# Splitting the first load of a row-wise kernel into three: runs of 2, 2 and 60 KiB instead of 2 and 62

## Chip, cores, metric

The kernel runs on one core of one Trainium2 chip. The metric is the device time of one execution in microseconds (us). All times are medians over several runs; profiles are of one execution each.

## What the kernel must compute

```python
# x: float32 [1024, 4096]
mean = np.mean(x, axis=-1, keepdims=True)
return ((x - mean) ** 2).astype(np.float32)
```

16.8 MB are read and 16.8 MB are written. The arithmetic is one sum and one square for each element.

## The kernel before

The 1024 rows are spread over 128 partitions and two tiles. A tile holds four rows on each partition, 64 KiB in one piece of memory. Both tiles have their own buffer, so no load waits for a buffer. All loads are issued first, on SP's queue; the first tile's load is cut in two, a "head" of 512 columns (2 KiB on each partition) and the remainder of 62 KiB.

```python
Q, HEAD = 4, 512                      # rows of a tile on a partition; columns of the head
x_t   = x.rearrange("(p n q) d -> n p (q d)", p=P, q=Q)
out_t = out.rearrange("(p n q) d -> n p (q d)", p=P, q=Q)

tiles = []
for i in range(ntiles):                                   # two tiles
    x_tile = io.tile([P, Q * D], F32)
    cuts = [0, HEAD, Q * D] if i == 0 else [0, Q * D]
    for lo, hi in zip(cuts, cuts[1:]):
        nc.sync.dma_start(out=x_tile[:, lo:hi], in_=x_t[i][:, lo:hi])
    tiles.append(x_tile)

for i in range(ntiles):
    ...   # means and squares in place, shared by ScalarE (ACT) and VectorE (DVE), 17 us a tile
    nc.sync.dma_start(out=out_t[i], in_=tiles[i])
```

## Time and profile before

| | before |
|---|---|
| time, median (first 3 runs) | 83.02 us (83.0 to 83.29) |
| profiled span | 81.4 us |
| DMA bytes, mean rate | 33.55 MB, 412 GB/s |
| DMA queue's share of 16 engines | 95.9% |
| VectorE, ScalarE busy | 41%, 43% |
| first tile landed | 22.51 us |

The prediction below shows the lines. How to read them: the share of the DMA queue is the time its packets took, over the span times 16 DMA engines. A packet here is one run of one partition: 2 KiB, 62 KiB or 64 KiB. In the views cut into 40 slices a packet is counted where it starts. "To landing" is from the start of a DMA's issue to its last semaphore update.

Besides the views I read the trace's packet records: start, duration and size of every packet. They do not name the engine. A packet of 4 bytes is the semaphore write with which an engine ends its part of a transfer, and an engine that goes straight on has its next packet 6 ns after it.

### The profile page before, as it was taken

How to read it: one execution, taken by the hardware profiler on the slowest of the kernel's cores; microseconds unless marked ns; L12 is line 12 of the kernel's file. 1: busy time of each engine (PE TensorE's matmuls, PEld its weight loads, DVE VectorE, ACT ScalarE, POOL GpSimd, SP SyncE). 2: the span in 40 equal slices, each digit the busy share in tenths (PEclk: the TensorE clock that was granted, in tenths of full speed). 3: DMA queues.
4: the chain of work that ended last, by engine and by line, in shares of the span. 5: the costliest groups of instructions: out<-in, count | busy, mean ns of one | idle time of the engine just before them, and what ended most of it. 6: DMA issues, size and time to landing. Idle time of an engine off the chain costs nothing.

```text
span 81.4 us, 83 instructions
## 1 busy us (share of the span) xinstructions
DVE 33.4 (41%) x16; ACT 34.7 (43%) x13; POOL 0.2 (0%) x4
## 2 busy tenths in 40 slices
DVE  0000000000089999999439999999900000000000
ACT  6000000000099999999339999999800000000000
POOL 0000000000000000000000000000000000000000
DMA  1999939999992999993899998399999199999290
GB/s 26 602 499 468 406 156 468 499 499 499 516 451 97 483 516 516 516 483 161 387 516 516 516 483 387 161 516 516 516 516 451 64 516 516 516 516 483 129 419 0
DMA packets 720, 33.55 MB, mean 412 GB/s; under 512 B 80, under 2 KB 80, under 8 KB 208
## 3 DMA queue, kind: packets, MB, share of 16 engines
q1 hardware_dynamic: 720, 33.55, 95.9%
HBM read 16.78 MB, written 16.78 MB: 412 GB/s over the span
## 4 chain that ended last, share of the span: by engine, by line
DMA 49%; DVE 21%; SPq 1%; issue 0%
DMA x_tile<-in_x_dram 49%; DVE neg_sum L67 16%; DVE x_tile L90 2%; DVE x_tile L89 1%; SPq L51 1%; DVE neg_mean L70 1%
## 5 line engine op out<-in xcount | busy, mean ns | idle before, releaser
L67 DVE TENSOR_REDUCE neg_sum<-x_tile 128x1 f32<-128x4096 f32 x6 | 26.5, 4412 | 25.0 <-DMA x_tile<-in_x_dram 25.0
L74 ACT ACTIVATE x_tile<-x_tile,neg_mean 128x4096 f32<-128x4096 f32 (+1 forms) x8 | 26.0, 3324 | 0.1
L59 ACT ACTIVATE copy<-x_tile 128x4096 f32<-128x4096 f32 x2 | 7.2, 3617 | 23.1 <-DMA x_tile<-in_x_dram 23.1
L90 DVE TENSOR_TENSOR x_tile<-x_tile 128x1792 f32<-128x1792 f32 x2 | 4.1, 2026 | 0.1
L89 DVE TENSOR_SCALAR x_tile<-x_tile,neg_mean 128x1792 f32<-128x1792 f32 x2 | 2.3, 1153 | 0.1
L59 ACT ACT_TABLE_LOAD x1 | 1.3, 1283 | 0.7 <-PEq L108 0.7
L70 DVE TENSOR_SCALAR neg_mean<-neg_sum 128x1 f32<-128x1 f32 x6 | 0.9, 154 | 0.2
L59 ACT ACTIVATION_READ_ACCUMULATOR copy<-x_tile 128x1 f32 x2 | 0.4, 186 | 0.0
L108 POOL MEMSET const-bfloat16-1.0<- 128x1 bf16 x1 | 0.1, 102 | 0.0
L108 POOL MEMSET const-uint8-127<- 128x1 uint8 x1 | 0.1, 101 | 0.0
L108 POOL MEMSET const-float32-0.0<- 128x1 f32 x1 | 0.1, 99 | 0.2 <-issue 0.2
L108 POOL MEMSET const-float32-1.0<- 128x1 f32 x1 | 0.1, 98 | 0.0
## 6 DMA issues: line engine op xcount, KB each, us to landing
x_tile<-in_x_dram SPq DMA_DIRECT2D x1, 7936.0 KB, 21.4
x_tile<-in_x_dram SPq DMA_DIRECT2D x1, 256.0 KB, 2.6
out_dram<-x_tile SPq DMA_DIRECT2D x2, 21.7
x_tile<-in_x_dram SPq DMA_DIRECT2D x1, 40.2
```

What stands on the lines that cost most here:

```text
L51: nc.sync.dma_start(out=x_tile[:, lo:hi], in_=x_t[i][:, lo:hi])
L59: nc.scalar.activation(out=copy, in_=row, func=ACT.Identity, scale=-inv_d, accum_out=neg_mean)
L67: inorder(nc.vector.reduce_sum(out=neg_sum, in_=row, axis=mybir.AxisListType.X, negate=True))
L70: inorder(nc.vector.tensor_scalar_mul(out=neg_mean, in0=neg_sum, scalar1=inv_d))
L74: inorder(nc.scalar.activation(out=part, in_=part, func=ACT.Square, bias=neg_mean, scale=1.0))
L89: nc.vector.tensor_scalar_add(out=back, in0=back, scalar1=m2)
L90: nc.vector.tensor_mul(out=back, in0=back, in1=back)
L108: nc = _bacc.Bacc("TRN2", target_bir_lowering=False, num_devices=1)
```

## The change

The intent is a longer run-in of small transfers before the big one. The bytes, the order and all compute stay as they are.

```diff
-        cuts = [0, HEAD, Q * D] if i == 0 else [0, Q * D]
+        cuts = [0, HEAD, 2 * HEAD, Q * D] if i == 0 else [0, Q * D]
```

The first tile has three loads: two heads of 2 KiB and a remainder of 60 KiB on each partition. The remainder is now the third issue on SP.

## The prediction

> **What bounds the kernel now.** I read the page first for busy shares, then the chain of waits, then the waits of SP's queue, and last the DMA view in short windows.
>
> The page, its slices and its DMA part:
>
> ```profile
> DVE 33.4 (41%) x16; ACT 34.7 (43%) x13; POOL 0.2 (0%) x4
> ...
> DVE  0000000000089999999439999999900000000000
> ACT  6000000000099999999339999999800000000000
> ...
> DMA  1999939999992999993899998399999199999290
> ...
> DMA packets 720, 33.55 MB, mean 412 GB/s; under 512 B 80, under 2 KB 80, under 8 KB 208
> ...
> q1 hardware_dynamic: 720, 33.55, 95.9%
> ```
>
> No compute engine is busy half of the span, while the one DMA queue fills 95.9% of the time of 16 DMA engines. 33.55 MB is x read once (16.78 MB) and the output written once. The low digits in the DMA row are an artefact: packets here last more than one slice and are counted where they start.
>
> The chain of waits, which starts from the last instruction (a VectorE one that ends at 58.8 us):
>
> ```profile
> 1.64 40.24 DMA x_tile<-in_x_dram
> 41.88 0.02 issue
> 41.90 4.43 DVE neg_sum L67
> ...
> 56.76 2.02 DVE x_tile L90
> ```
>
> Its chain runs through the second tile's load. It stops at 58.8 us and misses the last store, which the waits of SP's queue show:
>
> ```profile
> SPq L91 <- DVE x_tile L90: 55.0, 2, 36.1
> SPq L122 <- DMA out_dram<-x_tile: 21.2, 2, 19.3
> ```
>
> The program ends by waiting for the second store. The question is whether the DMA engines ever run dry before it. The timeline of SP's queue, with the landing times of the page's DMA issues, answers it:
>
> ```profile
> 0.73 1.33 SPq L51 DMA_DIRECT2D x_tile<-in_x_dram  x3
> 39.56 19.64 SPq L91 DMA_DIRECT2D out_dram<-x_tile  x2
> ...
> x_tile<-in_x_dram SPq DMA_DIRECT2D x1, 7936.0 KB, 21.4
> x_tile<-in_x_dram SPq DMA_DIRECT2D x1, 256.0 KB, 2.6
> out_dram<-x_tile SPq DMA_DIRECT2D x2, 21.7
> x_tile<-in_x_dram SPq DMA_DIRECT2D x1, 40.2
> ```
>
> Store 0 is issued at 39.56 us; the second load lands only at 41.88. Store 1 is issued at 58.85 (39.56 + 19.64, less its own 0.35); store 0 lands at 39.56 + 21.7 = 61.3. Each store is queued over 2 us before the transfer ahead of it has landed. So the four transfers follow each other without a hole, and the end is the first packet's time plus the sum of the packets on the slowest DMA engine. Compute can move by some tenths of a microsecond without moving the end.
>
> The speed inside a transfer comes from the DMA view of 5.1 to 21.4 us, where all packets are 62 KiB runs:
>
> ```profile
> DMA packets 112, 7.11 MB, mean 436 GB/s; under 512 B 0, under 2 KB 0, under 8 KB 0
> ...
> q1 hardware_dynamic: 112, 7.11, 100.6%
> ```
>
> 1.006 x 16.3 us x 16 engines / 112 packets = 2.342 us for 63,488 bytes, 27.1 bytes per ns on an engine, 434 GB/s on 16.
>
> The same view of 2.45 to 2.65 us, inside the first head:
>
> ```profile
> DMA packets 34, 0.07 MB, mean 348 GB/s; under 512 B 0, under 2 KB 0, under 8 KB 34
> ...
> q1 hardware_dynamic: 34, 0.07, 89.2%
> ```
>
> 0.892 x 0.2 us x 16 / 34 = 84 ns for 2,048 bytes, 24.4 bytes per ns. A short run costs a little over 10% more per byte than a long one.
>
> **What the Trainium skill says.** "DMA: Bandwidth & Descriptors", section "Where 436 GB/s comes from", puts the ceiling at 16 x 32 bytes x 850 MHz = 435 GB/s. The 434 GB/s above agrees: the long runs have nothing left to gain. The same page, "Why a DMA increments its semaphore by 16 and not by 1", says a tile of 128 partitions is spread over 16 engines, each with its own semaphore write. The trace agrees: 5 transfers and 80 packets under 512 B, 16 for each. The same page, "Latency and other measured facts", gives about 600 ns to a first byte for this kind of queue; the packet records put the first packet at 1.74 us, 0.63 us after the first issue ended at 1.11 us. "Perfetto Trace Analysis", section "DMA Optimizations", says that splitting DMAs may let work start sooner if the engines are generally idle. They are not idle here.
>
> **The change part by part.**
> 1. One more issue on SP. The three issues of loads stand at 0.73, 1.16 and 1.64 us (the chain of waits and the packet records' issue list agree), about 0.45 us apart. The big remainder of tile 0 is now issued third, at 1.64, not at 1.16. The first issue at 0.73 led to a first packet at 1.74, so 1.01 us; the remainder is ready at about 2.65 us. The second load moves to about 2.11 us, with nothing to do until some 21 us. Cost on the path: zero if the engines still have work at 2.65 us.
> 2. They have. The first head's closing semaphore writes lie at 2.66 to 3.01 us in the packet records. The second head, issued at 1.16 and so ready at about 2.2 us, follows with 8 packets of 84 ns on each engine: 0.67 us, to 3.3 to 3.7 us. The remainder has been waiting for 0.7 us or more by then.
> 3. 2 KiB of each partition move from a long run to a short one. On each engine: 8 x 84 ns = 672 ns for 16,384 bytes, against 16,384 / 27.1 = 604 ns before. That is +68 ns.
> 4. One more semaphore write on each engine, 9 ns in the packet records: +9 ns.
> 5. No compute instruction changes: the order of VectorE and ScalarE is the same. Tile 0 is still waited for as a whole by the first reduction (row 0 reaches past both heads) and by the mean of row 3, so the second head lets nobody start earlier.
>
> Sum on the path: 0.07 + 0.01 = **+0.08 us**, so 83.02 + 0.08 = 83.10 us.
>
> **Rivals.**
> - *A hole after the heads, because three issues come late.* For it: SP needs 0.45 us for each issue, and one head alone moves its steady part in 0.67 us an engine. Against it: step 2. If the remainder came up as late as 4 us there would be a hole of 0.3 to 0.6 us, and 83.4 to 83.7 us.
> - *A better start.* The first head runs at 220 GB/s on average from 1.7 to 2.66 us, and the first long packets average about 2.62 us in the packet records where later ones take 2.34: some 0.28 us is lost on each engine. If a longer run-in of short packets spared the long ones this, the time would be 82.8 to 82.9 us. For it: the existing head suggests that somebody found it worth having. Against it: the short packets already run at a steady 84 ns at the end of the first head, so nothing is left to warm up in the second; I expect the long packets' loss to be only moved later.
> - *Luck of the slowest engine.* The 16 engines end the first tile between 21.50 and 22.19 us and the last store between 79.67 and 80.21 us: the engine that lost most in its first long packet (2.99 us) plausibly stays last to the end. The mean of the last writes is 79.82, so the worst engine is 0.39 us behind. Another start deals this afresh: plus or minus 0.3 us.
> - *A store that misses its place.* Tile 0 landing later moves store 0's issue by as much, but also the second load. The store would be ready about 1.0 us after its issue, 40.6 us, and the first engine finishes the load at 40.84, the slowest at 41.58. The slack of the slowest, which sets the end, is 1 us. A delay of 0.08 on both sides takes nothing from it.
>
> **Range and chances.** The runs before span 83.0 to 83.29, so 0.3 us is noise or dealing of the start. Around 83.10 I take 0.25 below (the better start) and 0.4 above (a small hole, a worse slowest engine): 82.85 to 83.5. Two per cent is 1.66 us; no step above reaches half of it, so within 2% gets 0.98 and each side 0.01.
>
> **What would show it.** In the changed page: 864 packets (720 + 128 + 16), 96 under 512 B, 352 under 8 KB, a queue share still near 96%, a span near 81.5 us. Among the DMA issues: two of 256 KB landing about 2.6 and 2.9 us after issue, and one of 7680 KB about 21 us after its own. VectorE's first reduction starts near 22.7 us against 22.61. Store 0 is issued near 39.65. Steps 1 and 2 are wrong if no packet runs for some tenths of a microsecond between 2.7 and 4 us; step 3 is wrong if the second head's packets do not take about 84 ns; the second rival is right if the first long packets come close to 2.27 us (61,440 / 27.1) and tile 0 lands earlier than 22.5 us. The prediction as a whole fails if a store or the second load starts only after the engines have gone dry.

## The result

The changed kernel took **85.81 us** (85.35 to 85.86, 6 runs), the kernel before 83.16 (83.0 to 83.38, 6 runs). The ratio is 1.0304, 95% interval 1.0274 to 1.0335: slower by 3%. (A ratio here is the mean time of one kernel's runs over that of the other's of the same rounds, so not quite the ratio of the medians.) Executions over 1.5% slower than the fastest of the same kernel are left out of the means.

The changed kernel's page, its engine and DMA part:

```profile
DVE 33.4 (40%) x16; ACT 34.7 (41%) x13; POOL 0.2 (0%) x4
...
DMA packets 864, 33.55 MB, mean 399 GB/s; under 512 B 96, under 2 KB 96, under 8 KB 352
...
q1 hardware_dynamic: 864, 33.55, 94.3%
```

The packet counts are those predicted. Busy times of the engines are unchanged, and so is the work; only the span grew, from 81.4 to 84.0 us.

Its chain of waits, with the part that was shown of before:

```profile
1.64 0.42 SPq L51
2.06 0.04 issue
2.10 42.51 DMA x_tile<-in_x_dram
44.62 0.02 issue
44.64 4.43 DVE neg_sum L67
```

Its timeline of SP's queue, with the DMA issues of its page:

```profile
0.73 1.81 SPq L51 DMA_DIRECT2D x_tile<-in_x_dram  x4
42.35 19.59 SPq L91 DMA_DIRECT2D out_dram<-x_tile  x2
...
x_tile<-in_x_dram SPq DMA_DIRECT2D x1, 7680.0 KB, 23.6
x_tile<-in_x_dram SPq DMA_DIRECT2D x2, 256.0 KB, 2.8
out_dram<-x_tile SPq DMA_DIRECT2D x2, 21.6
x_tile<-in_x_dram SPq DMA_DIRECT2D x1, 42.5
```

Read against the lines of before: the remainder takes 23.6 us to land, where 62 KiB runs took 21.4. It is issued 0.47 us later too, so tile 0 is there at 1.64 + 23.63 = 25.27 us instead of 22.51. The second load lands at 44.62 instead of 41.88 (+2.74), and the last store, by the landing records, at 83.25 instead of 80.56 (+2.69). The stores take what they took. So the whole loss arises before 25 us, in the load of the first tile, and nothing later gives it back.

Now the start in a narrow window. This is the DMA view of the changed kernel from 3.8 to 5.6 us. Its second heads had ended on every engine by 3.745 us (last semaphore write in the packet records):

```profile
DMA  0000000000000090000900000000000990009900
...
DMA packets 7, 0.43 MB, mean 239 GB/s; under 512 B 0, under 2 KB 0, under 8 KB 0
```

Seven packets begin here: 0.43 MB / 7 = 61 KB, so they are long ones. The packet records give their starts as 4.43, 4.69, 5.23, 5.25, 5.28, 5.42 and 5.51 us. These are the first packets of the remainder on 7 of the 16 engines, which had nothing to do for 1.7 us on average: the last writes of their own heads lie at 3.16 to 3.60 us. The other nine went on without a gap at 3.20 to 3.75 us.

The same view of the kernel before, from 3.1 to 5.1 us (its head ends by 3.013 us):

```profile
DMA packets 0, 0.00 MB, mean 0 GB/s; under 512 B 0, under 2 KB 0, under 8 KB 0
```

No packet begins, because all 16 engines are inside the first long packet that they began at 2.67 to 3.02 us, each 5 to 6 ns behind its head.

There is a second symptom. The changed kernel from 5.8 to 9.3 us, when all engines have work:

```profile
DMA packets 19, 1.17 MB, mean 334 GB/s; under 512 B 0, under 2 KB 0, under 8 KB 0
...
q1 hardware_dynamic: 19, 1.17, 100.1%
```

1.001 x 3.5 us x 16 / 19 = 2.95 us for one packet of 60 KiB. Later the same packets take 2.267 us in the packet records. In this stretch the nine early engines are in their second packet, 3.43 us on average. The seven late ones spend 3.15 us on their first.

**The sum for the engine that ends last.** Before, its first long packet began at 2.82 us; after, at 5.51. Of this 2.68 us, 0.68 is the second head (8 x 84 + 9 ns), as predicted; **2.0 us is the hole**, by difference. Its eight long packets took 16.37 + 2.99 = 19.37 us before and 19.44 after: 8 x 0.075 = 0.60 less for the shorter runs, and **0.68 us more because more of them are slow** (1.33 us over the normal in sum, against 0.65). 0.68 - 0.60 + 2.0 + 0.68 = 2.76 us, which is the later landing of tile 0.

### The profile page after: what moved, and what is told of

Read it like the earlier page. It is cut to its first block, busy times and chain, and to the rows that moved or that the text cites. A ratio compares the mean times of both kernels' runs of the same rounds, so it can differ in the third digit from the quotient of the medians.

```text
span 84.0 us, 85 instructions
## 1 busy us (share of the span) xinstructions
DVE 33.4 (40%) x16; ACT 34.7 (41%) x13; POOL 0.2 (0%) x4
## 4 chain that ended last, share of the span: by engine, by line
DMA 51%; DVE 20%; SPq 1%; issue 0%
DMA x_tile<-in_x_dram 51%; DVE neg_sum L67 16%; DVE x_tile L90 2%; SPq L51 1%; DVE x_tile L89 1%; DVE neg_mean L70 1%
## 6 DMA issues: line engine op xcount, KB each, us to landing
x_tile<-in_x_dram SPq DMA_DIRECT2D x1, 7680.0 KB, 23.6
```

## The experiments

Each was run beside the kernel before on the same chip, with three rounds of timing. The diffs show the lines that matter, against the kernel before; those of e8 and e9 are against the changed kernel. A descriptor, in what follows, is the record of one run that a DMA engine is to move. An engine counts as late if its first long packet of the remainder begins after the last semaphore write of the short loads ahead of it. The first data of every run but e15 move at 1.73 to 1.81 us.

| run | remainder issued at, us | short loads end by, us | late engines | median, us | ratio to before (95%) |
|---|---|---|---|---|---|
| kernel before | 1.16 | 3.01 | 0 | 83.16 | |
| changed | 1.64 | 3.75 | 7 | 85.81 | 1.0304 (1.0274, 1.0335) |
| e16: changed again | 1.63 | 4.08 | 6 | 85.41 | 1.0259 (1.0200, 1.0319) |
| e1: one head, 4 KiB | 1.17 | 3.98 | 0 | 83.25 | 0.9996 (0.9914, 1.0077) |
| e2: second head issued third | 1.15 | 3.14 | 0 | 83.26 | 0.9986 (0.9921, 1.0051) |
| e9: second head on ACT's queue | 1.16 | 4.08 | 0 | 83.23 | 0.9984 (0.9918, 1.0049) |
| e11: one head, two runs | 1.21 | 4.18 | 0 | 83.59 | 1.0039 (1.0002, 1.0076) |
| e17: remainder delayed by half | 1.44 | 3.10 | 1 | 83.42 | 1.0055 (1.0015, 1.0096) |
| e14: remainder delayed | 1.70 | 3.09 | 14 | 84.82 | 1.0182 (1.0113, 1.0251) |
| e5: tiny load between | 1.55 | 3.14 | 2 | 85.39 | |
| e13: 2, 4, 58 KiB | 1.64 | 4.94 | 1 | 84.30 | 1.0133 (1.0095, 1.0172) |
| e15: tiny load first (data at 2.10) | 1.53 | 3.44 | 1 | 83.46 | 1.0048 (0.9969, 1.0127) |
| e7: 2, 14, 48 KiB | 1.63 | 7.63 | 0 | 83.06 | 0.9971 (0.9902, 1.0039) |
| e6: 14, 2, 48 KiB | 1.64 | 7.57 | 0 | 83.10 | 0.9971 (0.9891, 1.0050) |
| e8: second tile issued late | 1.63 | 3.76 | 9 | 85.41 | 1.0240 (1.0170, 1.0311) |

The count of late engines is a lower bound, because an engine whose own head ended early can wait before that last write. If each first long packet is paired with a semaphore write 5 to 6 ns before it, those left without a partner are 7 in the changed kernel, 7 in e16, 9 in e8, 15 in e14, 5 in e5, 3 in e15, 2 in e17 and one each in e13 and e2, none in the other rows. The one in e2 waited 0.17 us.

Not in the table, because their loads are not comparable: e0 (no head), e12, the first attempt at e14, and e19 (the three loads in mid-run).

### First call: is it the sizes, the number of loads, or the place of the remainder?

Theory A: the remainder is issued too late. Theory B: two heads fill what an engine's queue holds. Theory C: runs of 60 KiB are slow in themselves. Theory D: four outstanding loads are too many.

**e1_head_4k**

```diff
-        cuts = [0, HEAD, Q * D] if i == 0 else [0, Q * D]
+        cuts = [0, 2 * HEAD, Q * D] if i == 0 else [0, Q * D]
```

> One head of 4 KiB per partition, remainder issued second (60 KiB runs, as in the changed kernel). Theory A (the remainder is issued third, so its descriptors reach some DMA engines late, under load): no hole, 83.1 to 83.3 us. Theory B (the queue of a DMA engine holds few descriptors, and two heads of 8 fill it): no hole either, 8 descriptors ahead, 83.1 to 83.3. Theory C (60 KiB runs or a start of 4 KiB into the row are what runs slowly): 85.5 to 86.

Measured 83.25 us, the same as before. C is out: the remainder has the same 60 KiB runs from the same column, and each of its first packets takes 2.267 us (one 2.278).

**e2_head2_third** (the changed kernel's three loads, in another order)

```diff
+        parts = [(0, HEAD), (2 * HEAD, Q * D), (HEAD, 2 * HEAD)] if i == 0 else [(0, Q * D)]
```

> The changed kernel's three loads of tile 0, with the second head issued third, after the 60 KiB remainder. A and B: the remainder is second again, no hole, 83.1 to 83.4 us. C: 85.5 to 86. Theory D (four loads outstanding instead of three are too many, whatever their order): 85 to 86.

Measured 83.26 us, the same as before. D is out: all the loads of the changed kernel are there, 864 packets too. What helps is that the remainder is second.

**e4_one_dma_two_runs** (the 4 KiB head of e1, its access pattern written as two runs of 2 KiB)

```diff
+            if i == 0 and lo == 0:
+                to = to.rearrange("p (r c) -> p r c", c=HEAD)
+                of = of.rearrange("p (r c) -> p r c", c=HEAD)
```

> One head whose 4 KiB per partition are written as two runs of 2 KiB; if the access pattern is kept, the page shows 256 packets of 2 KiB and the DMA engines have 16 descriptors of data ahead of the remainder, as in the changed kernel, but one issue fewer. A: 83.1 to 83.3 us. B: a hole, 85 to 86 us. If the page shows 128 packets of 4 KiB, the pattern was merged and this run repeats e1.

Measured 83.37 us, but the page has 720 packets: the two adjacent runs were merged, so this repeats e1 and says nothing on B. e11 mends it.

**e5_tiny_between** (the kernel before, with a load of 512 bytes to one partition of a spare tile between head and remainder)

```diff
+            if i == 0 and lo == HEAD:
+                spare = scratch.tile([1, 128], F32)
+                nc.sync.dma_start(out=spare, in_=x[0:1, 0:128])
```

> The kernel before with a load of one partition and 512 bytes (one DMA engine, into a spare tile) issued between the head and the remainder: the remainder is issued third, at about 1.6 us, but 15 of 16 engines have only the first head's 8 descriptors ahead of it. A: late descriptors, some engines start the remainder past 4 us, 84.5 to 86 us. B: 83.1 to 83.4 us. D: 85 to 86 us.

Measured 85.53, 85.3, 83.62 and 85.47 us. The three higher runs lie over 1.5% above the fourth, so there is no ratio. The trace is of a high run (85.53); it has late engines, but there is no trace of the run at 83.62. Its DMA view from 3.2 to 4.5 us, after the last head ended at 3.14:

```profile
DMA packets 2, 0.13 MB, mean 98 GB/s; under 512 B 0, under 2 KB 0, under 8 KB 0
```

Two engines begin the remainder late, at 3.67 and 4.16 us. They are not the engine that had the extra transfer: in the packet records the 512-byte packet begins at 2.901, its semaphore write at 2.925 and a long packet at 2.931 us, without a gap. So one more transfer in an engine's own queue did not make that engine late, which speaks against B. What all engines share is a remainder issued at 1.55 us.

### Second call: how much must stand ahead of a remainder that is issued third?

**e6_long_short_rest**

```diff
+        cuts = [0, 7 * HEAD, 8 * HEAD, Q * D] if i == 0 else [0, Q * D]
```

> Three loads of tile 0 with runs of 14, 2 and 48 KiB. The remainder is issued third at 1.64 us, as in the changed kernel, but the first load keeps the engines busy to about 6 us. Theory B2 (a DMA engine's queue is supplied with two transfers at a time; the third is supplied only when the first is finished on it, and that takes 1 to 2 us): the 0.7 us of the second load do not hide it, so some engines idle about 1 us after it, near 6.5 to 8 us, and the time is 84.3 to 86 us. Theory A2 (the supply of the third transfer starts at its issue and is slow only beside the start of the others, done by 5.5 us): no hole, 83.1 to 83.4 us.

Measured 83.10 us, the same as before. The remainder's packets begin at 7.23 to 7.57 us, each right behind its engine's second load. B2 is out: here too the remainder is third and the load ahead of it is 2 KiB.

**e7_short_long_rest**

```diff
+        cuts = [0, HEAD, 8 * HEAD, Q * D] if i == 0 else [0, Q * D]
```

> Runs of 2, 14 and 48 KiB. The remainder is third, but the second load lasts some 4 us from 2.8 us on, longer than the late supply of the changed kernel (5.5 us at the latest). B2 and A2 both: no hole, 83.1 to 83.4 us. A theory that three loads of one tile, or four outstanding loads, cost 2.5 us in themselves: 85 to 86 us.

Measured 83.06 us, the same as before. Three loads of a tile cost nothing in themselves.

**e8_tile1_late** (the changed kernel, the second tile's load held back by a GpSimd fill of its buffer)

```diff
+        if i == 1:
+            nc.gpsimd.memset(x_tile[:, 0:2 * D], 0.0)
```

> The changed kernel, with the second tile's load issued only after a GpSimd fill of half of its tile (some us, to be landed long before 20 us). Theory F (the second tile's load, issued 0.45 us after the remainder, is what holds the remainder's supply back or slows its first packets): no hole and no slow packets, 83.1 to 83.4 us. B2 and A2: nothing changes, 85.3 to 86 us.

Measured 85.41 us. The second tile was issued at 7.68 us, and nine engines were late all the same, one of them by 0.07 us only (at 3.83 us). The DMA view of this run, 3.9 to 5.6 us, shows the other eight:

```profile
DMA  0000000000000000000009999990009000000000
...
DMA packets 8, 0.49 MB, mean 289 GB/s; under 512 B 0, under 2 KB 0, under 8 KB 0
```

All eight begin between 4.81 and 5.21 us, half of the engines in one group. The second tile's load has no part in it.

**e9_head2_on_act** (the second head on ScalarE's queue, at the same time as the first)

```diff
+            issuer = nc.scalar if lo == HEAD else nc.sync
+            issuer.dma_start(out=x_tile[:, lo:hi], in_=x_t[i][:, lo:hi])
```

> The second head is issued on ScalarE's queue, so the remainder is second on SP's. If the limit is two transfers in one issuing queue: no hole, 83.1 to 83.5 us. If it lies in the DMA engine over all queues: a hole, 84.5 to 86 us.

Measured 83.23 us, the same as before, no late engine. The remainder is second in SP's queue and is issued at 1.16 us.

### Third call: the count of descriptors, and the time that helps

**e11_one_dma_far_runs** (one head of two runs that cannot be merged: the first and the last 2 KiB of each partition's row of the tile)

```diff
+        cuts = [HEAD, Q * D - HEAD] if i == 0 else [0, Q * D]
+        if i == 0:
+            to = x_tile.rearrange("p (r c) -> p r c", c=HEAD)[:, 0:32:31, :]
+            of = x_t[i].rearrange("p (r c) -> p r c", c=HEAD)[:, 0:32:31, :]
+            nc.sync.dma_start(out=to, in_=of)
```

> One head in one load of two runs of 2 KiB per partition, the first and the last of the row of the tile, so they cannot be merged: 256 packets of 2 KiB, 16 data descriptors on each engine ahead of the remainder as in the changed kernel, but the remainder is the second load, issued at 1.16 us. A3: no hole, 83.1 to 83.4 us. B3 by the count of descriptors: a hole, 85 to 86 us.

Measured 83.59 us, ratio 1.0039. The packets are there (256 of 2 KiB), no engine is late. So 16 short packets an engine ahead of the remainder do no harm when the remainder is issued at 1.21 us. The median lies 0.2 us above the range I gave; two short runs instead of one add 0.08 us by the sum of the prediction, and the rest I did not look into.

**e13_2_4_58**

```diff
+        cuts = [0, HEAD, 3 * HEAD, Q * D] if i == 0 else [0, Q * D]
```

> Runs of 2, 4 and 58 KiB, so the two short loads keep the engines busy to about 3.9 to 4.4 us instead of 3.2 to 3.75. The remainder is issued third at 1.64 us as in the changed kernel. A3: if its descriptors reach the late engines at 4.4 to 5.5 us whatever comes before, the hole shrinks by 0.6 us but does not vanish, 83.7 to 85.2 us. If the late supply belongs to loads of 2 KiB runs only: 83.1 to 83.4 us.

Measured 84.30 us, ratio 1.0133: about half of the loss. The short loads last longer, to 3.90 to 4.94 us, and one engine is late, at 5.16 us, with a first packet of 3.24 us. A part of the supply still comes later than 5 us, and the more work stands ahead of it, the fewer engines notice.

**e0_no_head**

```diff
+        cuts = [0, Q * D]
```

> No head: tile 0 in one load of 64 KiB runs. It says what the first head of the kernel before is worth and whether first long packets are slow without short ones ahead. A3 and B3: no hole, since the first load is issued in an idle machine and the second has 20 us; 83.0 to 83.4 us.

Measured 83.07 us (82.97 to 83.1), ratio 0.9975 (0.9933, 1.0017). The head of the kernel before is worth nothing that these runs can see. Every first packet takes 2.95 to 3.34 us instead of 2.418, so the start loses 0.71 us on average. With a head it loses about as much: tile 0 ends on the average engine at 21.88 us here, at 21.83 in the kernel before.

**e14_rest_delayed** (the kernel before, the remainder held back by a GpSimd fill of 1024 of its columns)

> The kernel before (one head of 2 KiB, then the 62 KiB remainder), with the remainder's issue held back by a GpSimd fill of 1024 of its columns until about 1.64 us, which is when the changed kernel issues its remainder. Only two loads of tile 0, nothing between them. Theory A3 (what counts is when the remainder is issued: a transfer issued once the engines already move data gets its descriptors late, 2 to 4 us after issue on some engines, against 1 us in the kernel before): some engines start the remainder well after their head has ended at 2.5 to 3.1 us, up to 4 us, and the time is 83.6 to 85.6 us. Theory B3 (a third transfer or its descriptors do not fit the queue of an engine): starts right behind the head but for the 2.65 us that a fixed 1.01 us from issue gives, 83.1 to 83.3 us.

A miss: 101.77 us. The scheduler issued the second tile's load ahead of the held-back remainder, so tile 0 was there only at 41.96 us and compute began 20 us late. It does not answer the question, but it is a control for the next run, which keeps the order: with the same fill, the load that stands second was issued at 1.15 us, and one engine began it late, at 3.23 us (the head had ended by 3.07). So the fill by itself does not make most engines late.

### Fourth call: late, or third?

**e14_in_order** (only two loads of tile 0; the second is issued later)

```diff
+        if i == 0:
+            nc.gpsimd.memset(x_tile[:, HEAD:HEAD + 1024], 0.0)
         for lo, hi in zip(cuts, cuts[1:]):
-            nc.sync.dma_start(out=x_tile[:, lo:hi], in_=x_t[i][:, lo:hi])
+            tc.keep_in_program_order(
+                nc.sync.dma_start(out=x_tile[:, lo:hi], in_=x_t[i][:, lo:hi])
+            )
```

> As the run before with the delayed remainder, with the order of the loads kept: head, remainder held back to about 1.64 us by a GpSimd fill, second tile. The remainder is the second load in the queue. A3 (time of issue against the start of data): some engines start it well after their head's end at 2.5 to 3.1 us, up to 4 to 5 us; 83.6 to 85.6 us. T (third in the queue is what counts): at most the fixed 1.01 us from issue, so starts up to 2.7 us and behind the heads; 83.1 to 83.3 us.

Measured 84.82 us, ratio 1.0182. Its DMA view from 3.1 to 4.1 us (head ended by 3.087):

```profile
DMA  0909909090009090000000990000090900009000
...
DMA packets 14, 0.89 MB, mean 889 GB/s; under 512 B 0, under 2 KB 0, under 8 KB 0
```

Fourteen of 16 engines begin the remainder after the head has ended everywhere, up to 4.02 us, 1.3 to 2.3 us after its issue at 1.70. Their first packets take 3.05 us on average instead of 2.342. There is no second head here and no third load: **the later issue alone makes the effect**, at more than half of its size.

**e15_tiny_first** (three loads; the tiny one comes first, so that the head's data also start later)

```diff
+            if i == 0 and lo == 0:
+                spare = scratch.tile([1, 128], F32)
+                nc.sync.dma_start(out=spare, in_=x[0:1, 0:128])
```

> A load of one partition and 512 bytes first, then the head, then the remainder, then the second tile. The remainder is third, issued at about 1.6 us, but the head's data also start 0.4 us later, at about 2.15 us, so the remainder is issued as long before the data start as in the kernel before. A3: no late engine, the start is only 0.4 us later; 83.4 to 83.7 us. T: late engines, 85 to 86 us.

Measured 83.46 us (one run at 84.33), ratio 1.0048, which is the 0.4 us by which the head starts later. The DMA view from 3.45 to 5.5 us:

```profile
DMA packets 1, 0.06 MB, mean 31 GB/s; under 512 B 0, under 2 KB 0, under 8 KB 0
```

One engine is late by the table's count, at 3.78 us. The remainder is third and issued at 1.53 us, about as in e5, but its issue precedes the first 2 KiB packet by 0.57 us, as in the kernel before (0.58). In e5 it was 0.19, in the changed kernel 0.09. What counts is the time of the issue **against the start of the data**. The time from the issue to when an engine needs the remainder does not sort the runs: it was 1.5 to 1.9 us in the kernel before, with no late engine, and 1.5 to 2.1 us in the changed kernel, with seven.

**e12_few_descriptors** (two spare loads of 16 partitions with one 16 KiB run on each engine, then tile 0 whole)

> Two spare loads of 16 partitions and 16 KiB (one long packet on each engine from each, 2 x 262 KB more to move, 1.2 us at 434 GB/s), then tile 0 in one load, issued third at 1.64 us. The engines move data from 1.74 to about 3.1 us in long packets instead of 16 short ones. If short packets are what delays the third load: no late engines, 84.2 to 84.5 us. If any moving data does, or the third place in the queue: engines that start tile 0 at 4 us or later, 85.5 to 87.5 us.

Measured 87.24 us, but not for the reason in question. The first spare load's packets took 0.85 to 1.85 us, those of the second 2.17 to 2.41 us, most of them 2.407: 16 x 16,384 bytes in 2.407 us are 109 GB/s, a quarter of the usual rate. They ended only at 5.0 to 6.2 us. The Trainium skill, "SBUF — State Buffer", section "Door 1: The DMA port swizzle", gives about 109 GB/s as the limit of large transfers for a destination of partitions 0 to 15 (104 measured at 1 MiB); the second load's packets agree. Tile 0 followed on every engine within 34 ns, with first packets of 3.1 to 4.1 us. So whether short packets in particular delay the supply stays open.

**e16_changed_again**

> The changed kernel once more, on the chip of these runs: 85.3 to 85.9 us; 6 to 9 engines start the remainder between 4.4 and 5.5 us.

Measured 85.41 us, ratio 1.0259. Six engines begin at 4.1 to 5.4 us (DMA view, 4.1 to 5.6 us):

```profile
DMA packets 6, 0.37 MB, mean 246 GB/s; under 512 B 0, under 2 KB 0, under 8 KB 0
```

How many engines are late varies from trace to trace (7, 6, and 9 in e8), the time much less.

### Last call: how it grows, and whether it belongs to the start alone

**e17_delay_half** (as e14_in_order, with a fill of 704 columns)

> As the run with the delayed remainder in order, with a shorter fill: issue of the remainder at about 1.43 us, between 1.16 (kernel before) and 1.70. A3: first starts of the remainder at 2.6 to 3.4 us, a few engines late, 83.3 to 84.3 us, between the two. If the delay acts as a step (any issue after the data start is as late): 84.5 to 85 us. If only the fixed 1.01 us counts: 83.1 to 83.3 us.

Measured 83.42 us (83.24 to 84.02), ratio 1.0055: between the kernel before and e14. One engine is late, at 3.56 us. With the issue 0.58, 0.29 and 0.04 us ahead of the first packet (the kernel before, e17, e14) the loss is nothing, 0.5% and 1.8%: it grows steeply within half a microsecond.

**e19_three_in_mid_run** (tile 0 whole; the three loads with the second tile, held back by GpSimd fills until 20.58 us)

```diff
+        cuts = [0, Q * D] if i == 0 else [0, HEAD, 2 * HEAD, Q * D]
+        if i == 1:
+            tc.keep_in_program_order(nc.gpsimd.memset(x_tile[:, :], 0.0))
+            tc.keep_in_program_order(nc.gpsimd.memset(x_tile[:, 0:7100], 0.0))
```

> Tile 0 in one load; the second tile in the three loads of 2, 2 and 60 KiB, held back by GpSimd fills until about 20.7 us, so that the two heads run at 21.6 to 23 us and the remainder, issued at 21.6, follows. If any load issued beside moving data is late by 2 to 4 us: a hole of 1 to 2 us in the middle, 84.5 to 86.5 us. If lateness belongs to the start of the program alone (the stores reach idle engines 0.84 to 1.0 us after issue at 42 us in the traces so far): no hole, 83.1 to 83.5 us.

Measured 86.84 us, ratio 1.0465. The second tile landed at 45.38 us, 3.5 us later than in the kernel before. Its remainder was issued at 21.43 us. The DMA view from 23.2 to 26 us:

```profile
DMA  9999999994001019900009000000000000000000
```

The last digits of 9 are long packets that begin at 24.27, 24.35 and 24.73 us; the last of these is late (its 16 heads had all ended by 24.34). Over all 16 engines the first packet of the remainder takes 2.65 to 3.99 us, 3.33 on average, where the second takes 2.27 to 2.51. So slow first packets do not belong to the program's start alone: a load issued just in time beside full traffic is slow to get going in mid-run too. Late engines, which made most of the changed kernel's loss, are down to one here by the table's count, so that this is the same effect is not shown.

## Why the prediction was wrong

**Step 1 failed.** It said "The first issue at 0.73 led to a first packet at 1.74, so 1.01 us; the remainder is ready at about 2.65 us." The 1.01 us were measured on a load issued while no data moved. I carried them over to one issued 0.09 us before the first packet. In the changed kernel some engines had their first packet of the remainder 1.56 us after its issue, others only 2.8 to 3.9 us after it. With the issue held back by a GpSimd fill and no second head (e14) it was 1.3 to 2.3 us.

The trace of before could not have shown this, and I did not notice that it could not: its remainder always stood behind work. Its first packets at 2.67 us or later, issued at 1.16, say only that 1.5 us were enough there. What was right in step 1 was that the remainder is issued third at 1.64 us; that this would be free was the error.

**Step 2** was therefore wrong where it mattered. The heads ran as worked out (8 x 84 ns, ended by 3.745 us, and landings 2.8 us after issue in the median), but "the remainder has been waiting for 0.7 us or more by then" held on nine engines at most. The sign that I had named for an error in steps 1 and 2, that no packet runs for some tenths of a microsecond between 2.7 and 4 us, did not show, and would have missed the error: nine engines were busy all that time, and the hole was on the other seven.

**Steps 3 and 4** were right in size: 0.68 us for the second head's part of an engine, 0.60 us off the long packets, +0.08 in sum. They are the smallest terms of a sum whose largest ones, 2.0 us of hole and 0.68 us of slow packets on the engine that ends last, I had at zero.

**Step 5** was right: instructions, order and busy times are unchanged.

**The rivals.** The first one, a hole after the heads, is what happened. I bounded it by "as late as 4 us" and 0.6 us (with heads that end at 3.3 to 3.7 us it should have read 0.7); the last engine came at 5.51 us. The second rival, a better start, did not occur: first packets were not faster, and a kernel with no head at all is as fast (e0). Of the third, part is true: the engine that is behind after the start stays behind. On the first tile the last engine is 1.24 us behind the mean in the changed kernel (24.94 against 23.71 us), against 0.36 before. The fourth did not matter: store 0 was issued at 42.35 us, and the engines that had finished the second load from 42.15 us began it 0.85 to 1.0 us after issue, but the slowest finished the load only at 44.26.

**What stays open.** The records show late and slow first packets, not what held them. That descriptors reach the engines late when they are made beside moving data fits the runs, but is inferred. It does not by itself explain the second packets of 3.43 us on the nine early engines, at a time when the remainder had been issued for over 4 us. Nor do the runs tell short packets from long ones as the cause (e12 missed).

No version beat the kernel before: e0, e6 and e7 are the same within their intervals. The kernel before may sit near the edge itself: in e2, where the remainder is also issued second, one engine waited 0.17 us for it. Of its 35 runs, five took over 83.7 us (up to 86.1), and its remainder has half a microsecond to spare; no run shows that these are late engines.

## What to carry to other kernels

Issue first the transfer that will carry the time, or give it several microseconds of work ahead of it (work until 7.1 us was enough in e7, until 3.9 to 4.9 us not quite in e13): in a kernel that is bound by DMA from the first microsecond, half a microsecond of SP's issue time ahead of the big load cost 2.65 us, while the same loads in another order cost nothing. A latency read from an idle machine is not the latency of the next issue, and one that is always hidden in the trace has only an upper bound there. When a queue looks full on average (94% here), look at where packets begin in a narrow window after each short transfer.

## What the Trainium skill lacked or had wrong

- "DMA: Bandwidth & Descriptors", "Latency and other measured facts": the first byte after about 600 ns holds for the first issue (0.63 us from the end of issue). The row says nothing of an issue beside moving data, where first packets came 1.3 to 2.3 us after the start of the issue (e14) and up to 3.9 us (the changed kernel). With some engines idle, stores began 0.85 to 1.0 us after theirs (the changed kernel).
- "Perfetto Trace Analysis", "DMA Optimizations": it names splitting as a way to start sooner, and for small transfers an overhead of each, but not that a small load can make the large one behind it late. One more small load ahead of the large one cost 3.0% here; the same split with the large load issued second cost nothing (ratio 0.9986).
- No page that I read has it: the first long packets of a load issued just in time take longer than later ones of the same size, 3.33 us against 2.27 in mid-run (e19), 3.05 against 2.34 near the start (e14).
